# Seven products in the first up-projection pair of MLP groups 2 to 6, with low parts taken from a copy in PSUM

## The chip, the cores and the metric

The kernel runs on one core of one Trainium2 chip. The metric is the time of one execution on the device in microseconds; before the change three runs gave 1218.8, 1220.0 and 1220.02, with a median of 1220.0. The engines of the core are named as the profile names them: PE (TensorE: matmuls), PEld (its weight loads), DVE (VectorE), ACT (ScalarE), POOL (GpSimd) and SP (SyncE, which issues the loads).

## The reference

The program computes two layers of a decoder trunk on 512 tokens of width 1024, in float32. Layer 0 mixes tokens by attention with a forget gate, layer 1 by a gated short convolution. Each mixer is followed by a squared-ReLU MLP of inner width 4096 and by a gated embedding; RMSNorm stands around every part.

```python
D_MODEL = 1024; SEQ = 512; DEPTH = 2; D_FF = 4 * D_MODEL

def sq_relu_mlp(h, w_up, w_down):
    return jnp.square(jax.nn.relu(h @ w_up)) @ w_down

# in each layer i
x = x + rmsnorm(m, g[1])                                  # m: the mixer
f = sq_relu_mlp(rmsnorm(x, g[2]), w_mlp_up[i], w_mlp_down[i])
x = x + rmsnorm(f, g[3])
```

## The kernel before

**Split operands.** Each float32 operand is held as two tiles of a rounded type: `hi`, the value rounded by a cast on ScalarE (line 276), and `lo`, the rest, a subtraction on VectorE or GpSimd (line 277). One product is three matmuls into the same PSUM bank (`mm3`, lines 268 to 270): hi by hi, lo by hi, hi by lo. A weight tile of 128 x 512 thus costs a load, a cast and a subtraction before TensorE can use it.

**Groups.** The 4096 inner columns of an MLP are eight groups of 512. A group has four blocks f = 0 to 3 of 128 inner columns. Up: block f is 8 k steps of `mm3` with 512 moving columns (the tokens), 24 matmuls; ScalarE takes Relu and Square of the bank (lines 975 and 961). Group 0 does this in two halves of 256 tokens, since the tokens of its second half come out of the norm later. Down, in groups 0 to 6: seven products in place of eight, after Strassen and Winograd. `PRODUCTS` names the operand pairs, and `STEPS = (1, 2, 4, 5, 6, 7, 3)` their order. A operands (A11, A12, A22, S1 to S4) come from the squared blocks: blocks 0 and 1 give the parts p = 0, blocks 2 and 3 the parts p = 1. S1 and S2 share a tile, S3 and S4 another; their sums are GpSimd's (line 989), their casts ScalarE's, their low parts VectorE's. B operands are raw `w_down` tiles and the sums T1 to T4 of them; the sums are GpSimd's (line 168), and so are the low parts of T tiles from group 1 on. Each product has two banks, added to SBUF accumulators by VectorE (line 1021). Group 7 is plain.

**Weights.** All weight tiles stand in one list in the order of use. `prepare(upto)` issues the work for the list up to a place; a use of a tile calls it for `SOON` = 8 places ahead. Raw tiles arrive through a ring of 14 by DMAs on SP's queue; SBUF tiles of one size come from a ring of 70 pages, and PSUM is eight banks of 128 x 512.

**Order.** The program text is input to a scheduler that sets the order on each engine from its own estimates; only stretches under `manual_schedule` stand as written. On each engine the instructions run strictly in that order.

**Norm and convolution.** `pre_norm` computes statistics, scales the tokens, and puts off their transposition; then TensorE transposes into banks (`n_p`, line 337), ScalarE casts them into `hTh` and VectorE makes `hTl`. Between layer 0 and the convolution a function `quarters` copies each bank once more into float32 pages `B11`, `B21`, `B12`, `B22` (line 1242), from which the convolution makes token sums T1 to T4: its own projections c and b already run as seven products, with 256 moving columns (`sevens`).

## Time and profile before

| | |
|---|---|
| median of three runs | 1220.0 us (1218.8 to 1220.02) |
| span of the profiled execution, first to last instruction | 1216.5 us |
| around the span, to the median | 3.5 us |
| granted TensorE clock, mean | 0.999 |
| busy: PE, PEld | 1205.5, 1027.5 us |
| busy: DVE, ACT, POOL | 931.4, 691.4, 655.4 us |
| read from HBM | 139.03 MB |

The profile is of one execution, and its span is the profiled execution's own time as far as it is recorded; the runs' median is the time from outside. Busy time is the union of an engine's instructions. A matmul's end is modelled, and matmuls overlap: their cost is the distance between the starts of neighbours. In a group line the name left of the arrow is the tile that is written, right of it those that are read, without buffer numbers; then come count, total, mean in ns, and idle time before with what ended it. A timeline line gives start, length, engine, line, operation, tiles, count and, in brackets, the idle time before it and its releaser; a line with a count over 1 is a run of equal instructions.

### The profile page before, as it was taken

The numbers are of one execution on the slowest core, as the hardware profiler recorded it, in microseconds if no ns is written. First come the engines' busy times: TensorE is split into PE (matmuls) and PEld (weight loads), VectorE is DVE, ScalarE is ACT, GpSimd is POOL, SyncE is SP. The second block draws the span as 40 slices with busy tenths as digits, with TensorE's granted clock in tenths as the row PEclk, the third lists the DMA queues.
The fourth block names the chain that finished last, engine by engine and source line by source line (L and its number), as shares of the span: only waits on it lengthen the run. The fifth ranks groups of instructions, "written<-read, shape, count | busy, mean of one in ns | idle before, by whom it ended". The sixth has DMA issues, their size and how long they took to land.

```text
span 1216.5 us, 18743 instructions
## 1 busy us (share of the span) xinstructions
PE 1205.5 (99%) x6175; PEld 1027.5 (84%) x6175; DVE 931.4 (77%) x1474; ACT 691.4 (57%) x1465; POOL 655.4 (54%) x616
## 2 busy tenths in 40 slices
PE   9999999999999999999999999999999999999997
PEld 8888887898888888888889999989888888888886
DVE  7888889586669766879877888866876787669873
ACT  7687778458644564455665534545746445645551
POOL 2035666155787877774213455126676878678210
PEclk9999999999999999999999999999999999999999
DMA  9376544623234323438223123542422443135401
GB/s 333 122 210 172 167 152 125 222 93 94 77 113 138 102 66 110 139 97 276 83 88 108 35 80 103 176 154 71 139 87 65 127 138 106 61 112 185 162 13 58
DMA packets 87314, 150.84 MB, mean 124 GB/s; under 512 B 10352, under 2 KB 18080, under 8 KB 87216
## 3 DMA queue, kind: packets, MB, share of 16 engines
q1 hardware_dynamic: 86640, 149.11, 39.3%
q8 instruction: 49, 0.80, 0.3%
q10 hardware_dynamic: 576, 0.53, 0.1%
q14 instruction: 49, 0.40, 0.1%
HBM read 139.03 MB, written 6.37 MB: 120 GB/s over the span
## 4 chain that ended last, share of the span: by engine, by line
PE 91%; ACT 3%; issue 2%; DVE 2%; POOL 1%; DMA 0%; SPq 0%; POOLq 0%; DVEq 0%; ACTq 0%
PE up L269 9%; PE up L270 9%; PE up L268 9%; PE dn L268 8%; PE dn L270 8%; PE dn L269 8%; PE v L476 3%; PE pg L269 2%; PE pg L268 2%; PE pg L270 2%; PE qk L270 2%; PE qk L269 2%; PE qk L268 2%; PE pT L590 1%; PE co L269 1%
## 5 line engine op out<-in xcount | busy, mean ns | idle before, releaser
L277 DVE TENSOR_TENSOR wl<-raw,wh 128x512 fp32r<-128x512 f32 x346 | 344.7, 1041 | 14.1 <-ACT wh L276 13.4
L269 PE MATMUL up<-hTh,wl 128*128 128x512 f32 (+1 forms) x576 | 210.2, 365 | 0.0
L270 PE MATMUL up<-hTl,wh 128*128 128x512 f32 (+1 forms) x576 | 209.6, 365 | 0.0
L268 PE MATMUL up<-hTh,wh 128*128 128x512 f32 (+1 forms) x576 | 208.7, 366 | 0.0
L276 ACT CAST wh<-raw 128x512 fp32r<-128x512 f32 x346 | 189.4, 625 | 4.5 <-DVE xd L373 4.4
L975 ACT ACTIVATE r<-up 128x512 f32<-128x512 f32 (+1 forms) x72 | 39.5, 548 | 201.8 <-PE up L270 190.1
L277 POOL TENSOR_TENSOR wl<-dn_T,wh 128x512 fp32r<-128x512 f32 x96 | 132.7, 1416 | 30.0 <-ACT wh L276 30.0
L168 POOL TENSOR_TENSOR dn_T<-raw,raw 128x512 f32<-128x512 f32 x56 | 87.0, 1564 | 69.1 <-DMA raw<-in_wdn 50.5
L269 PEld LDWEIGHTS up<-hTh,wl 128*128 128x128 f32 x576 | 108.6, 189 | 17.5
L268 PEld LDWEIGHTS up<-hTh,wh 128*128 128x128 f32 x576 | 108.6, 189 | 17.5
L270 PEld LDWEIGHTS up<-hTl,wh 128*128 128x128 f32 x576 | 108.2, 189 | 17.4
L1021 DVE TENSOR_TENSOR acc<-dn,acc 128x512 f32<-128x512 f32 x168 | 107.4, 680 | 13.9 <-PE dn L270 13.9
L168 POOL TENSOR_TENSOR dn_T<-raw,dn_T 128x512 f32<-128x512 f32 x56 | 92.5, 1651 | 2.2
L276 ACT CAST wh<-dn_T 128x512 fp32r<-128x512 f32 x112 | 61.4, 616 | 10.9 <-POOL dn_T L168 10.9
L277 DVE TENSOR_TENSOR A12l<-q,A12h 128x512 fp32r<-128x512 f32 x28 | 23.2, 829 | 53.8 <-ACT A12h L276 53.8
L1035 POOL TENSOR_TENSOR acc<-acc,acc 128x512 f32<-128x512 f32 x28 | 46.9, 1707 | 9.9 <-DVE acc L1021 9.9
L277 DVE TENSOR_TENSOR A11l<-q,A11h 128x256 fp32r<-128x256 f32 x28 | 23.2, 828 | 36.5 <-ACT A11h L276 36.5
L270 PE MATMUL qk<-hTl,wh 128*128 128x512 f32 x128 | 50.7, 396 | 0.0
L269 PE MATMUL pg<-wh,hTl 128*128 128x512 f32 x128 | 50.5, 394 | 0.0
L268 PE MATMUL pg<-wh,hTh 128*128 128x512 f32 x128 | 50.4, 394 | 0.0
L268 PE MATMUL qk<-hTh,wh 128*128 128x512 f32 x128 | 50.3, 393 | 0.0
L269 PE MATMUL qk<-hTh,wl 128*128 128x512 f32 x128 | 50.2, 392 | 0.0
(404 smaller groups left out, 3304.5 us busy)
## 6 DMA issues: line engine op xcount, KB each, us to landing
raw<-in_wup SPq DMA_DIRECT2D x128, 256.0 KB, 2.9
raw<-in_wdn SPq DMA_DIRECT2D x128, 256.0 KB, 2.8
raw<-in_wcq SPq DMA_DIRECT2D x36, 256.0 KB, 2.8
raw<-in_wqk SPq DMA_DIRECT2D x32, 256.0 KB, 5.3
raw<-in_wpg SPq DMA_DIRECT2D x32, 256.0 KB, 4.1
g<-in_g SPq DMA_DIRECT2D x22, 256.0 KB, 5.9
prl<-neg_c SPq DMA_DIRECT2D x16, 256.0 KB, 6.3
raw<-in_wo SPq DMA_DIRECT2D x16, 256.0 KB, 4.7
```

The source lines that it names most:

```text
L168: ins = nc.gpsimd.tensor_tensor(out=B[name], in0=B[a], in1=B[b], op=op)
L268: nc.tensor.matmul(ps, a.hi, b.hi, start=start, stop=False)
L269: nc.tensor.matmul(ps, a.lo, b.hi, start=False, stop=False)
L270: nc.tensor.matmul(ps, a.hi, b.lo, start=False, stop=stop)
L276: nc.scalar.copy(hi, src)
L277: return eng.tensor_tensor(out=lo, in0=src, in1=hi.bitcast(F32), op=ALU.subtract)
L476: nc.tensor.matmul(ps[:, : V_CHUNKS[c][1]], getattr(of_x(k, t), p), getattr(ready["v", c, k], of), start=k == 0 and p == of, stop=k == KT ...
L590: nc.tensor.transpose(ps[:, b * P : (b + 1) * P], probs[h][b][:, j * P : (j + 1) * P], ident)
L975: nc.scalar.activation(r[:, :n], ps[:, :n], AF.Relu)
L1021: ins = nc.vector.tensor_tensor(out=a, in0=banks[s], in1=a, op=ALU.add)
L1035: nc.gpsimd.tensor_tensor(out=a, in0=a, in1=acc[i, s][:, :S], op=ALU.add)
```

## The change

In groups 2 to 6 of both layers blocks 0 and 1 of the up-projection are one product of a 1024 x 256 weight and the 1024 x 512 tokens, done as seven products of halves: seven times 4 k steps of `mm3` with 256 moving columns. The weight's forms are A11, A12, A22 raw and S1 to S4, summed by GpSimd with low parts on VectorE; the tokens' forms are quarters of hT and T1 to T4. The T tiles are made once per layer: `quarters` now also runs with the norm ahead of each MLP, and GpSimd subtracts, ScalarE casts and VectorE splits in groups 0 and 1, a step at a time between products. Two of the three banks are put together by four additions on VectorE, the third by ScalarE's half copy and one of them; `crossed` makes the A operands of the pair in its new layout.

In the same groups a weight's low part on VectorE is taken from a second rounded copy, which ScalarE writes to one of two PSUM banks (`beside`), kept for the rest of the layer's groups; S forms are left plain. T4 and T1 of `w_down` change from GpSimd to VectorE. The order of the T sums changes in all groups. Within groups 2 to 6 TensorE's order is as written, and the distance of preparation is set by hand. Pages are 77 in place of 70. The layout of the up weights of these pairs is permuted on the host.

```diff
-PAGES = 70
+PAGES = 77
+BESIDE = range(2, 7)
+ON_VECTOR = ("T4", "T1")
+PLAINLY = {("up", "S1"), ("up", "S2"), ("up", "S3"), ("up", "S4")}
+FIXED = range(2, 7)
+BACK = 6
+UP_SEVENS = range(2, 7)
+MORE = 0
+UP_FORMS = ("A11", "S2", "S1", "S3", "A12", "S4", "A22")
...
                 ((name, p), (a, p), (b, p), ALU.subtract)
+                for these in (
+                    (("T1", "B12", "B11"), ("T2", "B22", "T1"), ("T4", "B21", "T2")),
+                    (("T3", "B22", "B12"),),
+                )
                 for p in range(2)
-                for name, a, b in (("T1", "B12", "B11"), ("T3", "B22", "B12"),
-                                   ("T2", "B22", "T1"), ("T4", "B21", "T2"))
+                for name, a, b in these
...
                 eng = nc.gpsimd if (key[0] == "dn" and key[2] > 0) or key[-1] in ON_POOL else nc.vector
+                if key[0] == "up" or near(key) and key[3] in ON_VECTOR:
+                    eng = nc.vector
...
+            elif near(key) and eng is nc.vector and (key[0], key[-1]) not in PLAINLY:
+                split_beside(hi[:, :w], lo[:, :w], raw[:, :w], key[1])
             else:
                 split(hi[:, :w], lo[:, :w], raw[:, :w], eng)
...
+    def split_beside(hi, lo, src, l):
+
+        n = besides[l, "n"] = 1 - besides.get((l, "n"), 1)
+        if (l, n) not in besides:
+            besides[l, n] = bank(f"beside{l}_{n}")
+        copy = besides[l, n][:, : src.shape[-1]]
+        nc.scalar.copy(copy.bitcast(F32R), src)
+        nc.scalar.copy(hi, src)
+        nc.vector.tensor_tensor(out=lo, in0=src, in1=copy, op=ALU.subtract)
...
+                    if f < 2 and gr in UP_SEVENS:
+                        if f == 0:
+                            done(f, 0, S, *up_sevens(gr))
+                        continue
...
+                    if gr == 1:
+                        next(aside, None)
+                    if gr in FIXED:
+                        prepare(where["up", l, 2 * gr + 1, 3] + 1 + (SOON if f == 3 else SOON - BACK + 2))
...
+        def token_sums():
+            for name, a, b in (("T1", "B12", "B11"), ("T2", "B22", "T1"),
+                               ("T3", "B22", "B12"), ("T4", "B21", "T2")):
+                for q in range(2):
+                    full[name, q] = page(f"{name}f{l}_{q}")
+                    t = full[name, q][:, :S]
+                    nc.gpsimd.tensor_tensor(
+                        out=t, in0=full[a, q][:, :S], in1=full[b, q][:, :S], op=ALU.subtract
+                    )
+                    T[name, q] = Pair(*(page(f"{name}{s}{l}_{q}", F32R) for s in "hl"))
+                    split(T[name, q].hi[:, :S], T[name, q].lo[:, :S], t)
+                    yield
...
+        def up_sevens(gr):
+            L, R = slice(0, S // 2), slice(S // 2, S)
+            a, b, c = (bank(f"up{l}_{gr}_{s}") for s in "abc")
+            u, v, d, m = (page(f"u{s}{l}_{gr}") for s in "uvdm")
...
+            product(c[:, L], "A11", "B11")
+            nc.scalar.copy(u[:, L], c[:, L])
+            product(a[:, R], "S2", "T2")
+            product(b[:, L], "S1", "T1")
+            product(b[:, R], "S3", "T3")
+            product(a[:, L], "A12", "B21")
...
+            add(two(d[:, :S]), two(a), both(u[:, L]))
+            add(two(v[:, :S]), two(b), both(d[:, R]))
+            add(d[:, R], b[:, L], v[:, R])
+            product(c[:, L], "S4", "B22")
+            product(c[:, R], "A22", "T4")
+            add(m[:, :S], c, v[:, :S])
...
             for i in STEPS:
+                next(aside, None)
...
-            up(gr, done)
-            down(gr, A)
+            with ExitStack() as order:
+                if gr in FIXED:
+                    order.enter_context(tc.manual_schedule(engines={mybir.EngineType.PE}))
+                up(gr, done)
+                down(gr, A)
...
-            kind, lhs, xs, g1, lambda t: pre_norm(t, xs[t], g2, hT, f"n2{l}"), opened
+            kind, lhs, xs, g1, lambda t: pre_norm(t, xs[t], g2, hT, f"n2{l}", quarters), opened
```

**ScalarE at the end of the up-projection of group 5, layer 0.** `r`, `q` are Relu and Square of a block (the third number is f), `A11h` to `S3h` the casts of A operands, `wh` the casts of weights with the number of the place in the list; `dn_0_5_T4_1` is T4, p = 1. Before:

```order
L276 CAST wh190_6073<-dn_0_5_T4_0_5969 128x512
L276 CAST wh191_6083<-dn_0_5_T4_1_5977 128x512
L276 CAST wh192_6093<-dn_0_5_T1_0_5963 128x512
L276 CAST wh193_6103<-dn_0_5_T1_1_5971 128x512
L975 ACTIVATE r0_5_2_0_6113<-up0_5_2_0_6072 128x512
L961 ACTIVATE q0_5_2_5944<-r0_5_2_0_6113 128x512
L276 CAST A11h0_5_2_6116<-q0_5_2_5944 128x256
L975 ACTIVATE r0_5_3_0_6147<-up0_5_3_0_6122 128x512
L961 ACTIVATE q0_5_3_5945<-r0_5_3_0_6147 128x512
L276 CAST A12h0_5_3_6150<-q0_5_3_5945 128x512
L276 CAST S1h0_5_3_6158<-s120_5_3_6154 128x512
L276 CAST S3h0_5_3_6162<-s340_5_2_6120 128x512
```

Now:

```order
L1016 ACTIVATE r0_5_2_0_6508<-up0_5_2_0_6483 128x512
L996 ACTIVATE q0_5_2_6282<-r0_5_2_0_6508 128x512
L295 CAST A11h0_5_2_6511<-q0_5_2_6282 128x256
L1016 ACTIVATE r0_5_3_0_6542<-up0_5_3_0_6517 128x512
L996 ACTIVATE q0_5_3_6283<-r0_5_3_0_6542 128x512
L295 CAST A12h0_5_3_6545<-q0_5_3_6283 128x512
L295 CAST S1h0_5_3_6553<-s120_5_3_6549 128x512
L295 CAST S3h0_5_3_6557<-s340_5_2_6515 128x512
L311 CAST wh202_6561<-dn_0_5_T4_0_6371 128x512
L311 CAST wh203_6566<-dn_0_5_T4_1_6377 128x512
```

The casts of T4 and T1 stood ahead of block 2's Relu; now they stand behind block 3's last cast. Their copies to PSUM (not shown) stand ahead of the pair's Relus.

**VectorE at the same place, now.** `wl202` is the low part of T4, p = 0.

```order
L296 TENSOR_TENSOR A12l0_5_3_6546<-q0_5_3_6283,A12h0_5_3_6545 128x512
L1138 TENSOR_TENSOR acc0_1_1_4166<-dn0_5_11_6582,acc0_1_1_4166 128x512
L296 TENSOR_TENSOR S1l0_5_3_6554<-s120_5_3_6549,S1h0_5_3_6553 128x512
L296 TENSOR_TENSOR S3l0_5_3_6558<-s340_5_2_6515,S3h0_5_3_6557 128x512
L312 TENSOR_TENSOR wl202_6562<-dn_0_5_T4_0_6371,beside0_0_4698 128x512
```

These low parts of T4 were GpSimd's before; now they follow the last low part of the A operands on VectorE.

**ScalarE at the entry of the convolution.** `n0b_p` are the banks of the transposed tokens, `wh268` to `wh271` (`wh283` to `wh286` now) the weights of the second c and u, `cs` the first copy behind. Before:

```order
L276 CAST wh268_7869<-raw226_7871 128x512
L276 CAST wh269_7881<-raw227_7883 128x512
L276 CAST wh270_7893<-raw228_7895 128x512
L276 CAST hTh_84<-n0b_p2_0_7994 128x4x128
L276 CAST hTh_84<-n0b_p2_1_8005 128x4x128
L276 CAST wh271_7905<-raw229_7907 128x512
L276 CAST hTh_84<-n0b_p3_0_8016 128x4x128
L276 CAST hTh_84<-n0b_p3_1_8025 128x4x128
L927 COPY cs0_0_7942<-c0_0_7868 128x256
```

Now:

```order
L295 CAST hTh_84<-n0b_p2_0_8498 128x4x128
L295 CAST wh283_8373<-raw226_8375 128x512
L295 CAST hTh_84<-n0b_p2_1_8509 128x4x128
L295 CAST wh284_8385<-raw227_8387 128x512
L295 CAST hTh_84<-n0b_p3_0_8520 128x4x128
L295 CAST wh285_8397<-raw228_8399 128x512
L295 CAST hTh_84<-n0b_p3_1_8529 128x4x128
L295 CAST wh286_8409<-raw229_8411 128x512
L962 COPY cs0_0_8446<-c0_0_8372 128x256
```

Three of the four weight casts stood ahead of all the token casts; now one stands behind each token cast.

87 lines of the change are left out of this document (67 added, 20 removed).

## Prediction

> **What bounds the kernel now.** First I read the page: busy time by engine, and the chain that ended last.
>
> ```profile
> PE 1205.5 (99%) x6175; PEld 1027.5 (84%) x6175; DVE 931.4 (77%) x1474; ACT 691.4 (57%) x1465; POOL 655.4 (54%) x616
> PE 91%; ACT 3%; issue 2%; DVE 2%; POOL 1%; DMA 0%; SPq 0%; POOLq 0%; DVEq 0%; ACTq 0%
> ```
>
> Matmul spans overlap, so 99% alone proves little; the chain with 91% TensorE says more. Then I read the stages: two stretches of one steady group each in layer 0. The columns are length, then busy time (count) of PE, PEld, DVE, ACT and POOL, then clock, DMA share and GB/s.
>
> ```profile
> 399.00:440.00 41.00, 41.00 (x183) 33.96 (x182) 29.55 (x36) 21.03 (x39) 32.76 (x26) 1.00 0.33 104
> 440.00:481.00 41.00, 41.00 (x183) 33.96 (x182) 28.94 (x36) 21.03 (x39) 31.07 (x25) 1.00 0.34 103
> ```
>
> TensorE has no idle time here and its full clock, DMA is at a third, ScalarE at half and VectorE and GpSimd near three quarters. In groups 2 to 6, then, only fewer or cheaper matmuls shorten the kernel, as long as no other engine becomes late. What a matmul really costs is the distance between starts, read from the timeline: two starts 24 matmuls apart for 512 columns, and two starts 36 apart for 256.
>
> ```profile
> 433.84 0.39 PE L270 MATMUL up<-hTl,wh 128*128 128x512 f32 x1
> ...
> 439.28 0.39 PE L270 MATMUL up<-hTl,wh 128*128 128x512 f32 x1
> 439.51 0.39 PE L268 MATMUL dn<-wh,A11h 128*128 128x512 f32 x1
> ...
> 700.03 0.28 PE L268 MATMUL c_A<-T4h,wh 128*128 128x256 f32 x1
> ...
> 704.35 0.28 PE L268 MATMUL b_S<-T2h,wh 128*128 128x256 f32 x1
> ```
>
> 5.44 / 24 = 0.2267 us for 512 columns; 4.32 / 36 = 0.120 us for 256. A group has 96 matmuls up and 84 down: 180 x 0.2267 = 40.8 us.
>
> **The columns.** In ten groups (2 to 6, two layers) the first pair drops 48 matmuls of 512 columns and gains 84 of 256: 48 x 0.2267 - 84 x 0.120 = 10.88 - 10.08 = 0.80 us less. Seven eighths of the products would be 1.36 us; 256 columns cost more than half of 512, and that takes 0.56 back. Ten groups: **-8.0 us**. The 256-column rows are from the convolution's seven products, the same shape, with T tiles and with hT, and across a change of bank.
>
> **The work on the other engines.** The costliest groups of instructions give their prices, and three timeline rows the prices back to back.
>
> ```profile
> L277 DVE TENSOR_TENSOR wl<-raw,wh 128x512 fp32r<-128x512 f32 x346 | 344.7, 1041 | 14.1 <-ACT wh L276 13.4
> L276 ACT CAST wh<-raw 128x512 fp32r<-128x512 f32 x346 | 189.4, 625 | 4.5 <-DVE xd L373 4.4
> L1021 DVE TENSOR_TENSOR acc<-dn,acc 128x512 f32<-128x512 f32 x168 | 107.4, 680 | 13.9 <-PE dn L270 13.9
> L277 POOL TENSOR_TENSOR wl<-dn_T,wh 128x512 fp32r<-128x512 f32 x96 | 132.7, 1416 | 30.0 <-ACT wh L276 30.0
> L168 POOL TENSOR_TENSOR dn_T<-raw,dn_T 128x512 f32<-128x512 f32 x56 | 92.5, 1651 | 2.2
> ...
> 446.41 7.39 ACT L276 CAST wh<-raw 128x512 fp32r<-128x512 f32 x14
> 460.93 3.00 POOL L168 TENSOR_TENSOR dn_T<-raw,raw 128x512 f32<-128x512 f32 x2
> 463.83 5.21 DVE L277 TENSOR_TENSOR wl<-raw,wh 128x512 fp32r<-128x512 f32 x4
> ```
>
> Back to back a cast is 7.39 / 14 = 0.53 us, and a low part with both inputs in SBUF, beside GpSimd, 5.21 / 4 = 1.30. Each group's changes:
> - VectorE: three more low parts and four more from GpSimd (T4 and T1). Seventeen now read PSUM, 0.68 each by the accumulations' row, where ten cost 1.04: 17 x 0.68 - 10 x 1.04 = +1.2. The four S parts stay in SBUF: 4 x 1.04 = +4.2, less the four plain parts they replace, -4.2. Four additions from PSUM, +2.5. About 33 us of 40.
> - ScalarE: 17 copies and three casts, 20 x 0.53 = +10.6, and one half copy; 32 of 40.
> - GpSimd: four S sums, 4 x 1.65 = +6.6, less four low parts, 4 x 1.42 = -5.7; 33 of 40.
>
> All three fit below 40.0, so throughput costs nothing; the matmuls cover it, and without that cover VectorE's or GpSimd's 33 would be the bound. Two PSUM banks are held from group 2 on. Six remain; the seven products use three, a down product two, drained in 2 x 0.68 while the next takes 12 x 0.2267 = 2.7: free. DMA bytes are the same; SP's loads, at a third of the DMA time, cover a reordering. What remains is lateness in the queues.
>
> **T4's wait, each group.** T4's and T1's casts, ahead of block 2's Relu before, now stand behind S3h of block 3, and T4's low parts behind S3l on VectorE. The timeline of ScalarE and VectorE after the last up matmul (issue ends at 439.51):
>
> ```profile
> 439.71 0.60 ACT L975 ACTIVATE r<-up 128x512 f32<-128x512 f32 x1 [2.48 <-PE up L270]
> 441.00 0.62 ACT L276 CAST A12h<-q 128x512 fp32r<-128x512 f32 x1
> 442.98 0.62 ACT L276 CAST S1h<-s 128x512 fp32r<-128x512 f32 x1 [1.35 <-POOL s L989]
> 443.80 0.62 ACT L276 CAST S3h<-s 128x512 fp32r<-128x512 f32 x1 [0.20 <-POOL s L989]
> 444.33 2.18 ACT L276 CAST wh<-dn_T 128x512 fp32r<-128x512 f32 x4
> ...
> 445.45 1.42 DVE L277 TENSOR_TENSOR S3l<-s,S3h 128x512 fp32r<-128x512 f32 x1
> ```
>
> Product 4 starts 24 matmuls later, at 439.51 + 5.44 = 444.95. Its high part, cast at 444.33 in 0.62, lands at 444.95: just in time. The low part is used two matmuls later, at 445.40. S3h is there at 444.42; S3l takes 0.68 and blocks VectorE for 0.60 if GpSimd is quiet; T4's low part then runs from 445.05 to 445.73. TensorE waits 0.33 us, and everything down the group is queued behind. The ends: 0 if ScalarE runs earlier, and 1.0 if S3l takes 1.42 as in its row. I take 0.33, since GpSimd then waits for T2's cast, which stands still further back: 10 x 0.33 = **+3.3**. A12, wanted at 439.51 + 18 x 0.2267 = 443.59, is cast by 441.62 and its low part follows: covered.
>
> **Group 0, each layer.** The token sums need sixteen more ScalarE copies out of the transposes' banks. The first eight fall into ScalarE's wait for the norm (3.80 in the first row). The last eight stand behind block 2, and four banks stay taken.
>
> ```profile
> 255.91 0.64 ACT L312 ACTIVATE junk<-xb 128x512 f32<-128x512 f32 x1 [3.80 <-DVE xb L373]
> ...
> 268.89 3.18 POOL L168 TENSOR_TENSOR dn_T<-raw,dn_T 128x512 f32<-128x512 f32 x2
> 272.10 1.66 ACT L276 CAST wh<-dn_T 128x512 fp32r<-128x512 f32 x3 [5.71 <-POOL dn_T L168]
> 273.66 0.37 ACT L975 ACTIVATE r<-up 128x256 f32<-128x256 f32 x1
> ...
> 269.59 0.28 PE L268 MATMUL up<-hTh,wh 128*128 128x256 f32 x1
> ```
>
> ScalarE waits for T4's second half, GpSimd's eighth sum. The new order of the sums makes it the sixth, so block 2's Relu moves with it by 3.18, from 273.66 to 270.5. The block of matmuls that starts at 269.59 (48 x 0.120 before down) now needs that Relu's bank, free at 270.9, since the transposes' banks come later still, behind eight copies: **+1.3**, twice 2.6. Ends: 0 and 1.3 + 2.1, all eight copies (8 x 0.265: in the rows below two copies start 0.53 before the next two) on the path. The sixteen splits of the T tiles on ScalarE and VectorE and GpSimd's eight subtractions have groups 0 and 1 to hide in, product by product.
>
> **The convolution's entry.** Its source is the same, but ScalarE's order moved: three of the four weight casts that ran before the last transposes now stand between the hT casts.
>
> ```profile
> 649.41 1.65 ACT L276 CAST wh<-raw 128x512 fp32r<-128x512 f32 x3
> 652.94 1.08 ACT L276 CAST hTh<-n0b_p 128x512 fp32r<-128x512 f32 x2 [1.89 <-PE n0b_p L337]
> ...
> 657.73 0.68 ACT L1242 COPY B12f<-n0b_p 128x256 f32<-128x256 f32 x2
> 658.26 0.70 ACT L1242 COPY B22f<-n0b_p 128x256 f32<-128x256 f32 x2
> ```
>
> 1.65 us of filler leaves idle time and enters the path: **+1.6** (0 if TensorE has other work, 2.1 if all four casts count).
>
> **The sum.** -8.0 + 3.3 + 2.6 + 1.6 = -0.5 on a span of 1216.5. The runs' median, 1220.0, lies 3.5 above the span, so **1219.5 us**. This kernel's measurement tells nothing within about 0.2% (2.4 us) from no change.
>
> **The rivals.**
> *Relief, faster.* VectorE's low parts take one input from PSUM; if that frees GpSimd, whose sums take 1.65 us in the mean but 1.50 each in the row at 460.93, beside accumulations, ScalarE waits less for S1 and T4, and T4's and group 0's waits vanish: -8.0 + 1.6 = -6.4, **1213.6**. For it: the accumulations stay at 0.68 beside the same GpSimd. Against it: half of T4's wait is ScalarE's own chain, which GpSimd enters only once.
> The Trainium skill's page "ScalarE: Activation LUTs", section "Step-by-step: what each stage is for", holds that ScalarE writes faster to PSUM than to SBUF, with the caveat that TensorE should not need most of PSUM. No run here shows such a write; by that rule this rival gains, by the caveat the next one.
> *ScalarE late, slower.* The place is its queue from the first of the seven products to block 3's Relu. In 10.08 + 48 x 0.2267 = 20.96 us it does twenty copies and casts (10.6), a half copy and two Relus and Squares for the pair (2.7), the stretch from A12h to behind S3h (441.00 to 444.33 in the rows above, GpSimd's sums included: 3.3), and block 2's Relu, Square and A11 cast (1.7): 18.3, slack 2.7. Each copy into the two banks also waits until VectorE has read the one before. If the four S parts take 1.30 in place of 0.60 (+2.8) and 13 PSUM copies 0.625 in place of 0.53 (+1.2), the slack is overdrawn by 1.3 us, and from there each microsecond goes straight into T4's wait: 1219.5 + 13 = **1232.5**. For it: the 1.30 row. Against it: each of the rest reads PSUM.
> *The products don't shrink.* If weight loads set the pace at 1027.5 / 6175 = 0.166 us, the pair would cost 84 x 0.166 = 13.9, 3.1 more than now: **1258**. The 0.120 rows speak against it.
>
> **How the numbers follow.** Forecast 0.41, relief 0.30, ScalarE late 0.27, no shrinking 0.02. Each has its spread: relief in part ends inside the 0.2%, the forecast's own ends reach outside. Faster 0.31, same 0.40, slower 0.29. The forecast's own range is 1216 to 1223; the range for 8 in 10 reaches to relief and to most of late ScalarE: 1213 to 1231.
>
> **What would show it.** Groups 2 to 6 should take 40.3 us each, with a hole of some 0.3 us on TensorE two matmuls into product 4, released by VectorE's low part. No hole at all, and GpSimd's sums near 1.3, would be relief. Holes at the first product's second half, or at S4's product (which waits until ScalarE has copied the bank's left half), and Relu of block 3 starting late, would be late ScalarE. Group 0 should show a wait of PE for a Relu near its third late block, and the convolution's entry an idle stretch of 1 to 2 us before the second c and u. A pitch over 0.120 in the products would refute the first term; TensorE idle for raw tiles from DMA would refute what I hid.

## The result, and the profile after

The changed kernel takes **1255.4 us** (median of four runs, 1253.8 to 1256.5) against 1220.0: a ratio of **1.0296**, 95% interval 1.0281 to 1.031. It is 35 us slower; the forecast was 1219.5, with a range of 1213 to 1231. The profiled execution has a span of 1254.8, 38.3 more than before.

The page of the changed kernel, busy time by engine and the chain that ended last:

```profile
PE 1219.3 (97%) x6535; PEld 1039.1 (83%) x6535; DVE 959.6 (76%) x1600; ACT 814.9 (65%) x1723; POOL 669.6 (53%) x632
PE 51%; DVE 14%; ACT 12%; POOL 11%; issue 8%; DMA 3%; POOLq 0%; SPq 0%; DVEq 0%; ACTq 0%
```

No engine became the bound: the fullest after TensorE (PE and its weight loads) is VectorE at 76%. But PE's share of the chain fell from 91% to 51%: it now waits in turn for three engines that are each idle for about a quarter of the time or more. To find where, I read the start of each group's first up matmul from the timelines of both kernels and took the lengths between them:

| stretch (us) | before | after | difference | forecast |
|---|---|---|---|---|
| start to group 0, layer 0 | 250.6 | 252.2 | +1.6 | 0 |
| groups 0 to 3, layer 0 | 167.2 | 181.2 | +14.0 | +0.4 |
| groups 4 to 6, layer 0 | 122.4 | 124.5 | +2.1 | -1.4 |
| group 7 to layer 1's group 0 | 278.9 | 283.2 | +4.3 | +1.6 |
| groups 0 to 3, layer 1 | 166.7 | 179.6 | +12.9 | +0.4 |
| groups 4 to 6, layer 1 | 122.4 | 125.6 | +3.2 | -1.4 |
| group 7, layer 1, to the end | 108.4 | 108.5 | +0.1 | 0 |

(The forecast column is the prediction's terms put into these stretches: per layer 1.3 for group 0, and per group of 2 to 6 0.33 less 0.80.) So 27 of the 38 us are lost in groups 0 to 3, 22 of them in groups 0 and 1, before the first seven products are reached. The windows view, first of before for groups 0 and 1, then of after for groups 0, 1 and 4, with the columns as in the prediction:

```profile
250.60:295.30 44.70, 44.57 (x293) 40.20 (x292) 30.57 (x38) 29.16 (x65) 23.17 (x23) 1.00 0.22 73
295.30:333.90 38.60, 38.60 (x172) 31.95 (x172) 29.38 (x32) 27.15 (x51) 30.24 (x24) 1.00 0.35 107
```

```profile
252.20:303.30 51.10, 45.74 (x293) 40.28 (x292) 40.02 (x44) 39.07 (x93) 34.86 (x30) 1.00 0.18 57
303.30:349.10 45.80, 42.57 (x182) 33.36 (x181) 23.59 (x37) 23.25 (x44) 40.69 (x29) 1.00 0.30 93
...
433.40:475.00 41.60, 41.16 (x218) 34.69 (x217) 32.39 (x48) 31.28 (x59) 28.93 (x25) 1.00 0.32 100
```

Group 0 does the same 293 matmuls in 51.1 us instead of 44.7, and VectorE, ScalarE and GpSimd each have some ten us more there. In group 1 PE idles 3.2 us while VectorE and ScalarE are idle for half of it; GpSimd is shown busy for 40.7 of 45.8 us, which the experiments take apart. (Before, two us of group 2 are drawn forward into group 1, so its 38.6 compare with about 40.8.) What PE waited for in the changed kernel, in total, times, and longest:

```profile
PE dn L289 <- DVE wl L296: 7.1, 8, 1.1
PE dn L287 <- ACT wh L311: 3.0, 10, 0.6
...
PE dn L287 <- ACT A11h L295: 2.5, 2, 1.4
PE up L287 <- ACT r L1016: 2.5, 4, 1.5
```

The first row, eight waits for plain low parts, is group 0's products with S1 and S3; the second, ten waits, one in each group with seven products; the last is the wait forecast for group 0. Behind some of these waits TensorE's granted clock falls as well (last section).

### The profile page after: what moved, and what is told of

It is laid out like the page before. It is cut to its first block, busy times and chain, and to the rows that moved or that the text cites. A ratio compares the mean times of both kernels' runs of the same rounds, so it can differ in the third digit from the quotient of the medians.

```text
span 1254.8 us, 19832 instructions
## 1 busy us (share of the span) xinstructions
PE 1219.3 (97%) x6535; PEld 1039.1 (83%) x6535; DVE 959.6 (76%) x1600; ACT 814.9 (65%) x1723; POOL 669.6 (53%) x632
## 4 chain that ended last, share of the span: by engine, by line
PE 51%; DVE 14%; ACT 12%; POOL 11%; issue 8%; DMA 3%; POOLq 0%; SPq 0%; DVEq 0%; ACTq 0%
PE dn L289 4%; PE dn L288 4%; PE dn L287 4%; DVE wl L312 4%; POOL s L1091 3%; DVE wl L296 3%; POOL dn_T L179 3%; POOL s L1108 3%; DVE acc L1138 3%; PE v L511 2%; PE qk L289 2%; PE qk L288 2%; PE qk L287 2%; ACT q L996 2%; DMA raw<-in_wup 2%
## 5 line engine op out<-in xcount | busy, mean ns | idle before, releaser
L296 DVE TENSOR_TENSOR wl<-raw,wh 128x512 fp32r<-128x512 f32 x206 | 173.7, 884 | 10.7 <-ACT wh L295 10.4
L287 PE MATMUL up<-hTh,wh 128*128 128x512 f32 (+1 forms) x416 | 148.1, 358 | 2.5 <-ACT r L1016 2.5
L288 PE MATMUL up<-hTh,wl 128*128 128x512 f32 (+1 forms) x416 | 147.8, 357 | 0.0
L289 PE MATMUL up<-hTl,wh 128*128 128x512 f32 (+1 forms) x416 | 147.3, 356 | 0.0
L310 ACT CAST beside<-raw 128x512 fp32r<-128x512 f32 x130 | 74.9, 587 | 40.5 <-DVE wl L312 38.5
L312 DVE TENSOR_TENSOR wl<-raw,beside 128x512 fp32r<-128x512 f32 x130 | 84.3, 679 | 12.6 <-ACT beside L310 11.4
L296 POOL TENSOR_TENSOR wl<-dn_T,wh 128x512 fp32r<-128x512 f32 x56 | 71.7, 1314 | 40.0 <-ACT wh L295 40.0
L287 PEld LDWEIGHTS up<-hTh,wh 128*128 128x128 f32 x416 | 78.6, 189 | 14.4 <-ACT r L1016 3.3
L288 PEld LDWEIGHTS up<-hTh,wl 128*128 128x128 f32 x416 | 78.6, 189 | 10.9
L296 DVE TENSOR_TENSOR A11l<-q,A11h 128x256 fp32r<-128x256 f32 (+1 forms) x28 | 21.2, 759 | 51.7 <-ACT A11h L295 51.7
L296 DVE TENSOR_TENSOR wl<-up_S,wh 128x512 fp32r<-128x512 f32 x40 | 51.2, 1293 | 0.0
```

The lines of the kernel that those rows point to most:

```text
L287: nc.tensor.matmul(ps, a.hi, b.hi, start=start, stop=False)
L288: nc.tensor.matmul(ps, a.lo, b.hi, start=False, stop=False)
L289: nc.tensor.matmul(ps, a.hi, b.lo, start=False, stop=stop)
L296: return eng.tensor_tensor(out=lo, in0=src, in1=hi.bitcast(F32), op=ALU.subtract)
L310: nc.scalar.copy(copy.bitcast(F32R), src)
L312: nc.vector.tensor_tensor(out=lo, in0=src, in1=copy, op=ALU.subtract)
```

## The experiments

The theory at the start (A): the token sums, which I had priced at nothing, cost most of it, in groups 0 and 1. The rival (B): the steady groups, with ScalarE late. All times below are medians against 1219.3 to 1219.7 for the kernel before on the same chip (1220.0 for the changed kernel); the last three columns are read as in the table above, the groups as the sum of both layers, in the kernel's profiled execution.

| kernel | us | ratio, 95% interval | groups 0-3 | groups 4-6 | between layers |
|---|---|---|---|---|---|
| before | 1219.3 to 1219.7 | 1 | 333.9 | 244.8 | 278.9 |
| changed | 1255.4 | 1.0281 to 1.031 | 360.8 | 250.1 | 283.2 |
| order_only | 1221.1 | 1.0005 to 1.0023 | 332.5 | 244.8 | 281.8 |
| beside_only | 1222.3 | 1.0014 to 1.0033 | 332.6 | 242.6 | 283.6 |
| sevens_free | 1230.2 | 1.0071 to 1.0102 | 335.6 | 250.0 | 283.3 |
| sums_only | 1248.0 | 1.022 to 1.025 | 358.0 | 244.8 | 283.6 |
| sevens_only | 1331.1 | 1.0901 to 1.0934 | 387.3 | 299.5 | 282.5 |
| copies_only | 1234.4 | 1.011 to 1.014 | 342.5 | 244.8 | 282.1 |
| copies_own | 1222.2 | 1.0011 to 1.0031 | 335.8 | 244.8 | 280.1 |
| sums_nosplit | 1234.8 | 1.011 to 1.0144 | 346.2 | 244.8 | 283.3 |
| casts_only | 1235.7 | 1.0108 to 1.0145 | 346.6 | 244.8 | 283.3 |
| lows_pool | 1256.8 | 1.0293 to 1.0324 | 367.5 | 244.8 | 282.1 |
| sums_vector | 1251.4 | 1.0252 to 1.0291 | 359.1 | 248.7 | 281.9 |
| splits_later | 1253.0 | 1.0251 to 1.0286 | 358.4 | 250.9 | 282.7 |
| vector_later | 1247.0 | 1.0203 to 1.0235 | 351.3 | 249.9 | 281.8 |
| all_group1 | 1260.5 | 1.0318 to 1.0349 | 367.2 | 251.1 | 282.7 |
| from3 | 1261.2 | 1.0326 to 1.0357 | 367.7 | 248.6 | 281.8 |
| beside_all | 1262.6 | 1.034 to 1.0375 | 372.2 | 248.1 | 283.3 |
| after_own | 1247.1 | 1.0209 to 1.0241 | 357.7 | 249.0 | 280.4 |
| own_vector_later | 1241.2 | 1.0165 to 1.0199 | 350.0 | 249.2 | 279.8 |

### Which part of the change costs

**The token sums alone.**

```diff
-UP_SEVENS = range(2, 7)
+UP_SEVENS = range(0)
-BESIDE = range(2, 7)
+BESIDE = range(0)
-FIXED = range(2, 7)
+FIXED = range(0)
```

with the old order of GpSimd's weight sums.

> The kernel before, with the sixteen copies of the turned tokens and the eight token sums per layer with their splits made and thrown away: plain products and plain splits everywhere, and the old order of GpSimd's weight sums. Theory A (the token sums, made in groups 0 and 1, cost most of the 35 us, because GpSimd's sums there hold up VectorE's low parts and VectorE's stream then holds up GpSimd): the changed kernel's own marks moved by 13.0 and 12.2 us over groups 0 and 1 of the two layers, so this one loses some 20 to 27 us, 1240 to 1247 us, and a GpSimd sum of over 5 us stands in group 1. Rival B (the steady groups with the seven products and the second copy lose it, ScalarE being late): nothing of theirs is in it, so it loses no more than the 2.6 us forecast for group 0 and some 3 us at the convolution's entry, 1220 to 1226 us.

Measured 1248.0, just above theory A's range. Copies, sums and splits that nothing uses cost 28 us in a kernel that is otherwise the one before but for its ring of 77 pages, and all of it lies in groups 0 to 3 and around them; groups 4 to 6 are to the tenth as before. A GpSimd sum of over 8 us is there too.

**Seven products and token sums without the second copy.**

```diff
-BESIDE = range(2, 7)
+BESIDE = range(0)
```

> The changed kernel without the second rounded copy in PSUM: all low parts are made from the two SBUF inputs as before, and the T4 and T1 weight sums and the seven products' sums keep their engines of before where the new branch does not ask for VectorE. Theory A: the token sums' 25 us stay, the steady groups come within 2 us of the changed kernel's either way, 1240 to 1265 us. Rival B: ScalarE loses 130 copies of 0.59 us, which is 76 us of its work, and the steady groups fall from 41.5 to 40.3 us, so about 12 us come back, 1238 to 1245 us, with groups 0 and 1 unchanged at 12 us lost.

Both were wrong: 1331.1. The second copy does not slow the sevens down, it carries them; without it groups 2 to 5 take 48 to 50 us each and group 6 takes 52.7, and PE waits in each for ScalarE's cast of A11. ScalarE is late there because it waits for VectorE's additions (the second row, from group 4 of layer 0, where ScalarE is busy for 23.2 of 49.2 us):

```profile
PE dn L287 <- ACT A11h L295: 30.9, 10, 3.1
...
464.87 0.63 ACT L1077 ACTIVATE rd<-ud 128x512 f32<-128x512 f32 x1 [12.04 <-DVE ud L1053]
```

The edit also gives the low parts of T4 and T1 back to GpSimd, so the run does not test the second copy alone.

**The second copy alone.**

```diff
-UP_SEVENS = range(2, 7)
+UP_SEVENS = range(0)
-FIXED = range(2, 7)
+FIXED = range(0)
-        aside = token_sums()
+        aside = iter(())
```

and no copies of tokens.

> The kernel before with the second rounded copy alone: VectorE's low parts of groups 2 to 6 read PSUM, no seven products in the up-projection, no copies of tokens and no token sums. Theory A: 0 to 4 us faster or the same, 1214 to 1222 us, since PE was 97 per cent busy and sets the steady groups' 40.8 us. Rival B: ScalarE's added copies make high parts late in each group, 0.5 to 1.2 us in each of ten groups, 1225 to 1232 us.

1222.3, between the two. The groups are no longer than in order_only; what it lost lies between the layers and goes with the next run, not with ScalarE. (Of its 283.6 there 1.8 are group 7's, whose first matmuls are drawn forward into group 6.)

**What is left of the edit.** As the last one, with BESIDE empty as well.

> The changed kernel's file with no seven products, no second copy, no copies of tokens and no token sums: what is left are the new order of GpSimd's four weight sums for the down-projection, 77 pages instead of 70 and the smaller scratch for transfers. It prices the rest of the edit. Both theories hold it to be nothing: within 2 us of before, 1218 to 1222 us. If it were the cause of the 3 to 5 us lost between the layers, 1223 to 1226 us.

1221.1, as expected, though not quite nothing. Groups 0 to 3 even gain 1.4 us over both layers, and 2.9 are lost between them, at the convolution's entry, where ScalarE's order is that of the changed kernel (more on it below). All kernels with a ring of 77 pages have 281.8 to 283.6 there, those with 69 pages (below) 279.8 to 280.4, the one before, with 70, 278.9. That the ring brings the order is suggested by this list, and no run has isolated it. Beside_only aside, every kernel above 282.1 has a stretch at half the granted clock in this part, and no other has one.

**Sevens and second copy without the token sums.**

```diff
-                return T[name, k // 2].at(lambda u: u[:, k % 2 * 256 : k % 2 * 256 + 256])
+                return hT.at(lambda u: u[:, k, : S // 2])
-        aside = token_sums()
+        aside = iter(())
```

and no copies of tokens. The sums are left out, so the result of the up-projection is another.

> The changed kernel without the copies and the token sums: the products with T1 to T4 read the first half of the first four chunks of the turned tokens in their place (left out: the sums, so the up-projection's result is another). Everything of groups 2 to 6 stays. If groups 0 and 1 alone lose what the ladder says, groups 0 and 1 come back to the 82 us of the run with the new order alone, the steady groups keep 41.4 to 41.6 us against 40.8, and it takes 1225 to 1233 us. If the steady groups themselves are held up by what groups 0 and 1 leave late, they fall to 40.3 us as forecast, 1214 to 1219 us.

1230.2. Taken as steps from the kernel before to the changed one, the 35 us are 1.4 for the order, 1.2 more for the second copy (the two intervals overlap), 7.9 more for the seven products, and 25.1 more for the token sums with their copies. What speaks for the last step is that it comes out alike in two kernels: in groups 0 to 3 the token sums cost 360.8 - 335.6 = 25.2 us in the changed kernel, and 358.0 - 333.9 = 24.1 without any seven products, with the old order of the weight sums. Two questions remain: what in the token sums costs 25 us, and why a steady group takes 41.5 and not 40.3.

### The token sums, step by step

**The copies.** From sums_only, with the sums left undone:

```diff
-        aside = token_sums()
+        aside = iter(())
```

> The first step of a ladder up to the run with the token sums alone (1247.95 us): the kernel before with the sixteen copies of the turned tokens on ScalarE per layer, nothing made of them. Both theories: the changed kernel entered group 0 1.6 us later and its group 0 waited 1.65 us for a bank behind the copies, so 2 to 4 us per layer, 1222 to 1227 us.

1234.4: sixteen copies per layer of some 0.3 us each cost 15 us, where both theories gave 2.5 to 7.5. The timeline of this kernel, PE first, then ScalarE:

```profile
272.53 0.28 PE L286 MATMUL up<-hTl,wh 128*128 128x256 f32 x1
276.52 0.39 PE L284 MATMUL up<-hTh,wh 128*128 128x256 f32 x1 [3.71 <-ACT r L1013]
...
262.33 2.05 ACT L292 CAST hTh<-n_p 128x512 fp32r<-128x512 f32 x4 [2.45 <-PE n_p L369]
...
274.53 1.66 ACT L292 CAST wh<-dn_T 128x512 fp32r<-128x512 f32 x3 [5.60 <-POOL dn_T L176]
276.10 0.38 ACT L1013 ACTIVATE r<-up 128x256 f32<-128x256 f32 x1
...
277.26 0.64 ACT L1331 COPY B12f<-n_p 128x256 f32<-128x256 f32 x2
```

The four banks of the transposes are read by the casts at 262.33, and ScalarE could be done with them at 264.4. The copies read them as well, and stand in ScalarE's queue at 277.26, behind casts that wait 5.60 us for GpSimd. So four of eight banks stay taken for some 13 us more, PE runs out of banks at 272.6, and what it then waits for is a Relu in that same queue. ScalarE waited for GpSimd before too (5.71 us in the prediction's row); with eight banks PE did not feel it. Behind this hole the granted clock is at half from 277.9 to 281.3, so group 0 loses more than the hole: it takes 49.9 us in place of 44.7.

**The same copies, early.**

```diff
-                full[at] = page(f"{at[0]}f{q}")
+                full[at] = normed.tile([P, S], F32, tag=f"{at[0]}f{q}", name=f"{at[0]}f{q}_{l}")
-PAGES = 77
+PAGES = 69
```

> The run with the copies alone, but the copies go to eight pages of their own instead of pages of the ring (which has 69 then instead of 77). In ScalarE's queue the second half's eight copies then stand right behind the casts that read the same four PSUM banks, and no longer behind four weight casts that wait 5.6 us for GpSimd. Theory of the banks (the copies, late in the queue, hold four of eight banks from 262 to 278 us, so PE has to wait 3.9 us for a Relu that stands in that queue too): the hole of 3.9 us goes, group 0 comes from 49.9 back to 44 to 46 us, 1222 to 1228 us. Rival (ScalarE's time for sixteen copies, wherever they stand, or the ring of pages): 1231 us or more.

1222.2: 12 of the 15 us are back. ScalarE's timeline of this kernel:

```profile
262.66 0.66 ACT L1331 COPY B12f<-n_p 128x256 f32<-128x256 f32 x2
...
274.44 1.66 ACT L292 CAST wh<-dn_T 128x512 fp32r<-128x512 f32 x3 [4.50 <-POOL dn_T L176]
276.00 0.38 ACT L1013 ACTIVATE r<-up 128x256 f32<-128x256 f32 x1
```

The same Relu is as late as in the last run (276.00 against 276.10), and PE waits for no Relu any more: with the copies right behind the casts the banks are free. It is the banks, and not ScalarE's time, that cost. (Order and ring change together in this run; the rows speak for the order.)

**The sums, without their splits.** From sums_only:

```diff
-                    T[name, q] = Pair(*(page(f"{name}{s}{l}_{q}", F32R) for s in "hl"))
-                    split(T[name, q].hi[:, :S], T[name, q].lo[:, :S], t)
                     yield
```

> The second step of the ladder: copies and GpSimd's eight token sums per layer, no casts and no low parts of them. Theory of the shared memory port (a GpSimd sum and VectorE's low parts take turns, 1.73 us for the pair instead of 0.60 and 1.29): eight sums cost VectorE about 9 us per layer where it has none to spare, so half or more of the ladder's 28 us is here, 1234 to 1243 us. Theory of ScalarE's order (a cast that waits for its sum holds the casts and copies behind it): no cast waits for a sum here, so at most 2 us above the copies alone, 1224 to 1229 us, and the third step, the splits, costs the rest.

1234.8: GpSimd's eight sums add 0.4 us to the copies by the medians (2.5 by the spans of the two profiled executions). The theory of the shared memory, in this form, falls: half of the 28 us was to be here. That 1234.8 lies in its range is luck, since the copies alone cost more than both theories gave.

**The casts, without the low parts.** From sums_only:

```diff
-                    split(T[name, q].hi[:, :S], T[name, q].lo[:, :S], t)
+                    nc.scalar.copy(T[name, q].hi[:, :S], t)
```

> Between the ladder's second step (copies and sums, 1234.8 us) and its third (with casts and low parts, 1248.0 us): the eight casts per layer on ScalarE, without VectorE's eight low parts. If ScalarE's order is the price (each cast waits for its sum and holds two weight casts and two accumulator copies behind it): 1244 to 1248 us. If it is VectorE (eight more operations with two SBUF inputs where GpSimd's sums and weight low parts take turns already): 1235 to 1239 us.

1235.7: 0.9 more. So the last step of the ladder, eight low parts of 0.6 us per layer on VectorE, costs the other 12 us.

**The low parts on GpSimd.** From sums_only:

```diff
-                    split(T[name, q].hi[:, :S], T[name, q].lo[:, :S], t)
+                    split(T[name, q].hi[:, :S], T[name, q].lo[:, :S], t, nc.gpsimd)
```

> The run with the token sums alone (copies, sums, casts and low parts, unused: 1248.0 us), the eight low parts per layer by GpSimd instead of VectorE. If VectorE's own queue is the price (three low parts per product there at up to 1.73 us each, 5.2 us against 2.72 us of PE), VectorE is back to two per product, the holes of 3.0 us at S1 and S3 in group 0 shrink below 1.2 us and the time falls to 1236 to 1241 us. If it is the shared memory, whoever makes them, or GpSimd's queue, in which the weight sums of group 1 now stand behind eight more operations, nothing or less than 3 us is gained: 1245 to 1255 us.

1256.8, the rival, and above its range. VectorE had its two low parts per product again, and group 0 fell from 53.6 to 51.7 us; but group 1 rose from 41.9 to 48.5. The timelines of the three say why. Casts only, VectorE, GpSimd and ScalarE:

```profile
297.92 19.52 DVE L293 TENSOR_TENSOR wl<-raw,wh 128x512 fp32r<-128x512 f32 x14
...
302.34 1.42 POOL L176 TENSOR_TENSOR dn_T<-raw,raw 128x512 f32<-128x512 f32 x1 [1.49 <-PE dn L286]
...
317.99 1.47 POOL L1029 TENSOR_TENSOR T4f<-B21f,T2f 128x512 f32<-128x512 f32 x1
...
319.49 0.62 ACT L1033 CAST T4h<-T4f 128x512 fp32r<-128x512 f32 x1 [5.46 <-POOL T4f L1029]
```

All token sums, low parts on VectorE:

```profile
297.90 3.46 DVE L293 TENSOR_TENSOR wl<-dn_T,wh 128x512 fp32r<-128x512 f32 x2
...
309.11 3.70 DVE L293 TENSOR_TENSOR wl<-raw,wh 128x512 fp32r<-128x512 f32 x6
...
305.76 9.43 POOL L176 TENSOR_TENSOR dn_T<-raw,raw 128x512 f32<-128x512 f32 x2 [4.95 <-DVE T3l L293]
...
323.76 1.29 POOL L1029 TENSOR_TENSOR T4f<-B21f,T2f 128x512 f32<-128x512 f32 x1
...
325.08 0.62 ACT L292 CAST T4h<-T4f 128x512 fp32r<-128x512 f32 x1 [8.46 <-POOL T4f L1029]
325.60 0.59 ACT L1013 ACTIVATE r<-up 128x512 f32<-128x512 f32 x1
```

Low parts on GpSimd:

```profile
313.79 3.44 POOL L176 TENSOR_TENSOR dn_T<-raw,raw 128x512 f32<-128x512 f32 x2
...
327.45 1.26 POOL L1029 TENSOR_TENSOR T4f<-B21f,T2f 128x512 f32<-128x512 f32 x1
...
328.75 0.62 ACT L292 CAST T4h<-T4f 128x512 fp32r<-128x512 f32 x1 [10.60 <-POOL T4f L1029]
```

The last of the eight token sums stands on GpSimd behind the eight weight sums of group 1, and its cast on ScalarE in front of the second Relu of group 1. The cast starts 16.2, 19.2 and 25.8 us after group 1's first matmul (303.29, 305.87 and 302.98), and group 1 takes 38.9, 41.9 and 48.5 us: us for us. The low parts put GpSimd's weight sums back: on GpSimd they stand ahead of them (the sums begin at 313.8 in place of 302.3), and beside them on VectorE the first of the sums takes 8.2 us (last section). The token sum moves with the weight sums, then its cast, the Relu, and what stands behind that: A12's cast, the casts of group 1's weight sums and GpSimd's low parts of these. PE feels it in the down part of group 1, by 4.44 us at A12's cast in lows_pool, and by 1.1 at GpSimd's low parts in both kernels that are late. The rest, in group 0, is VectorE: with three low parts per product at up to 1.73 us each (the 3.46 for two above) against 2.72 us of PE, PE waits there for plain low parts, 5.1 us in sums_only over both layers.

The changed kernel has the same rows, GpSimd and ScalarE:

```profile
302.76 8.65 POOL L179 TENSOR_TENSOR dn_T<-raw,raw 128x512 f32<-128x512 f32 x1 [4.49 <-PE dn L288]
...
322.86 0.62 ACT L295 CAST T4h<-T4f 128x512 fp32r<-128x512 f32 x1 [8.82 <-POOL T4f L1032]
323.39 0.59 ACT L1016 ACTIVATE r<-up 128x512 f32<-128x512 f32 x1
```

The Relu at 323.39 stands behind a cast that waits 8.82 us and whose result nobody needs before group 2.

### Other places for the same steps

**The sums on VectorE.** From the changed kernel:

```diff
-                    nc.gpsimd.tensor_tensor(
+                    nc.vector.tensor_tensor(
                         out=t, in0=full[a, q][:, :S], in1=full[b, q][:, :S], op=ALU.subtract
```

> The changed kernel with the eight token sums per layer computed by VectorE instead of GpSimd, all else as it is. Theory A in its narrow form (the two engines hold each other up at the memory they share, two-input sums on GpSimd against two-input low parts on VectorE): the four holes of 4.2 us in all at group 0's products with S1 and S3 shrink below 1.5 us, the GpSimd sum of 8.65 us falls below 3 us, and 10 to 22 us come back, 1233 to 1245 us. The rival (it is the amount of work in groups 0 and 1, above all ScalarE's casts in their place in its queue): under 5 us come back, 1250 us or more.

1251.4: of the narrow theory's two signs both came (PE waits for no low part at S1 and S3, and the sum of 8.65 us is gone), and of its 10 to 22 us only 4, which is the rival's figure. Now ScalarE waits for VectorE's sum in each step:

```profile
290.27 0.62 ACT L295 CAST T1h<-T1f 128x512 fp32r<-128x512 f32 x1 [0.55 <-DVE T1f L1032]
...
293.46 0.62 ACT L295 CAST T2h<-T2f 128x512 fp32r<-128x512 f32 x1 [0.56 <-DVE T2f L1032]
```

3.19 us from step to step, where PE needs 2.72 for a product. Group 0 falls to 47.3, group 1 rises to 49.0.

**The splits in group 1.** Eight sums in group 0, then two splits after each block of group 1:

```diff
                 next(aside, None)
+                if i == STEPS[0]:
+                    next(aside, None)
...
                     if gr == 1:
                         next(aside, None)
+                        next(aside, None)
```

with `token_sums` giving first all sums, then all splits.

> The changed kernel with GpSimd's eight token sums still stepped through group 0's products (all eight there now), but their casts and low parts only in group 1, two after each of its four up-projection blocks. Two mechanisms for the four holes of 4.2 us at group 0's products with S1 and S3 are told apart. If it is ScalarE's order (a cast that waits for its sum stands ahead of the product's two weight casts and two copies; with the sums on VectorE such a step took 3.19 us against 2.72 us of a product), the holes go and group 0 comes down from 51 to about 47 us. If it is the memory that VectorE and GpSimd share (weight low parts at 1.73 us instead of 0.60 while a token sum runs, two of them per product), the holes stay at 3 to 4 us. Either way the T4 cast no longer stands ahead of group 1's Relus, which is worth up to 7 us per layer: 1236 to 1248 us.

1253.0, above the range. Group 0 falls to 48.6 and keeps 1.8 us of holes at S1 and S3, half of what it had: both mechanisms are in them. Group 2 then waits for what group 1 has not done, 46.6 instead of 42.8 us.

**The same, sums on VectorE.** From the last run:

```diff
-                    nc.gpsimd.tensor_tensor(
+                    nc.vector.tensor_tensor(
```

> As the run with the later splits, but the eight sums by VectorE in group 0. Neither of the two mechanisms has a place in group 0 here: no cast waits for a sum there and GpSimd is still, so both theories want group 0 within 1.5 us of the 44 us of before plus the 2 us of its copies, with no hole over 0.4 us at S1 and S3. What is left of the loss in group 1 tells what the splits cost there: 1228 to 1240 us. If more than 15 us per layer pair stay lost in groups 0 and 1, both mechanisms are too small and the casts' and low parts' sheer amount is the cause.

1247.0, above the range. Group 0 is as forecast by both, 45.6 us with no hole at S1 or S3. But groups 1 and 2 take 43.3 and 45.6, and 8.4 us are won where 15 or more were to be.

**Everything in group 1.**

```diff
-                next(aside, None)
                 a_name, b_name = PRODUCTS[i]
...
                         next(aside, None)
+                        next(aside, None)
```

> The changed kernel with all of the token sums, casts and low parts in group 1, two whole steps after each up-projection block, none in group 0. Theory of ScalarE's order: group 0 comes back to about 46 us (the copies alone), and group 1 becomes the slow one, since its Relus now stand behind casts that wait for GpSimd's sums, which stand behind eight weight sums: group 1 at 50 us or more, 1248 to 1262 us. Rival (the amount of work decides, and group 1 has room, as ScalarE has no accumulator copies there): both groups together lose under 4 us per layer, 1230 to 1240 us.

1260.5, as the theory of ScalarE's order had it: 51.0 us in group 1, and 46.6 in group 0.

**Sevens from group 3, steps in groups 1 and 2.**

```diff
-UP_SEVENS = range(2, 7)
+UP_SEVENS = range(3, 7)
...
-                    if gr == 1:
+                    if gr in (1, 2):
                         next(aside, None)
...
-                next(aside, None)
                 a_name, b_name = PRODUCTS[i]
```

> The changed kernel with seven products from group 3 instead of 2, and the token sums stepped one after each up-projection block of groups 1 and 2, none in group 0: half of them now run where VectorE's low parts read PSUM. If room is what counts (groups 0 and 1 have none on VectorE and ScalarE, the steady groups have 9 us on each), groups 0 to 3 fall from 181 to 171 to 174 us per layer: 1234 to 1243 us. If the order of the steps counts (each a round trip of sum, cast and low part in front of a Relu), each of the eight steps costs 1.5 us wherever it stands: 1248 us or more.

1261.2, the rival. Room does not help: half of the steps now stand in group 2, of a kind in which VectorE and ScalarE are idle for a quarter of the time or more (26.0 and 30.6 of 40.8 us busy in beside_only), and group 2 takes 50.0 us.

**The second copy in groups 0 and 1 too.**

```diff
-BESIDE = range(2, 7)
+BESIDE = range(0, 7)
```

> The changed kernel with the second rounded copy in PSUM in groups 0 and 1 too, so that VectorE's low parts of weights there no longer read two SBUF operands. Theory of the port: VectorE's low parts stay at 0.6 to 0.7 us beside GpSimd's sums, the stretch of 8.65 us is gone, and groups 0 to 3 fall from 181 to about 172 us per layer, 1235 to 1246 us. Theory of ScalarE: it gets some 30 more copies of 0.59 us in groups 0 and 1 of each layer, 18 us, in the order that already held them up: groups 0 to 3 rise to 185 us or more, 1260 to 1290 us.

1262.6, as the theory of ScalarE had it. PE's longest waits are for banks again, two of which are now the copies':

```profile
PE n_p L372 <- ACT r L1016: 8.7, 2, 4.4
PE up L287 <- ACT r L1016: 6.5, 2, 4.2
```

### The two findings put to use

**Copies in pages of their own, in the changed kernel.** The edit of copies_own:

```diff
-                full[at] = page(f"{at[0]}f{q}")
+                full[at] = normed.tile([P, S], F32, tag=f"{at[0]}f{q}", name=f"{at[0]}f{q}_{l}")
```

> The changed kernel with the copies in eight pages of their own, the ring having 69 pages. Theory of the banks: the hole of 1.65 us in group 0 goes and the loss before it shrinks, 3 to 8 us back in both layers together, 1247 to 1252 us, since here the hole was already smaller than in the run with the copies alone. Rival (the ring of pages is what is short, since sixteen pages of split token sums live through five groups): eight pages fewer in it cost more than that gains, 1256 us or more.

1247.1, 8.3 us back, at the edge of what was expected: 3.1 in groups 0 to 3, 2.8 between the layers, 1.4 ahead of group 0, 1.1 in groups 4 to 6.

**With later splits and the sums on VectorE as well**, the edits of vector_later on top:

```diff
-                    nc.gpsimd.tensor_tensor(
+                    nc.vector.tensor_tensor(
...
                     if gr == 1:
                         next(aside, None)
+                        next(aside, None)
```

> The changed kernel with what the runs found put right as far as possible: copies in pages of their own (8.3 us in the changed kernel), the eight sums by VectorE in group 0 and the splits after group 1's blocks (8.4 us). If the two are separate causes they add up: 1255.4 - 8.3 - 8.4 = 1238.7, so 1236 to 1242 us. If they were the same loss counted twice (PE waiting in groups 0 and 1 for whatever comes last), no more than 2 us is gained over the better one: 1244 to 1248 us. Not below 1230 us in either case, which is what the steady groups cost without any token sums.

1241.2 for the 1238.7 of the sum: 14.2 of the 25 us that the token sums cost are back, and the two causes are mostly separate. It is the best form of the change that was run, and still 1.8% slower than the kernel before. With 1230 for the sevens without any token sums, I do not expect any placing of these alone to win.

## Why the prediction was wrong

**The step that failed** is the price of the token sums: 2.6 us for their copies, and nothing for the rest, because the sixteen splits of the T tiles and GpSimd's eight subtractions "have groups 0 and 1 to hide in, product by product". Together they cost 25 of the 35 us. Alone in the kernel before, the copies cost 15, and the sums, casts and low parts that were priced at nothing 13.5 more. How the 25 us of the changed kernel divide between the two is not isolated; 8.3 come back when only the copies move, 8.4 when only the sums and splits do, 14.2 with both. I looked at room, in the steady groups (33, 32 and 33 us of 40), and for these steps neither at the room in groups 0 and 1 nor at order. The steps are round trips of GpSimd, ScalarE and VectorE, spliced into queues that run strictly in order, with Relus and weight casts behind them; the ladder shows that sums and casts by themselves cost 1 us, and the low parts 12 or 21, by the queue in which they make others late. The part of my own working that asks what is queued behind a wait was done for T4's weights and for the copies, and not for the sums and splits.

**Group 0's copies.** Place and mechanism were right: PE waits for a Relu behind block 2, with four banks still taken. Forecast 1.3, measured 1.65 in layer 0 of the changed kernel (the earlier GpSimd sum does help: 3.9 without it); in layer 1 PE waits there twice, 0.33 each. But the banks had a second price that I did not look for; after_own gave 8.3 us in all where the term had 2.6, though the 2.8 of them between the layers may be the ring's, and some 1.3 of these the clock's, since after_own has no stretch at half clock there.

**The columns.** Right: 84 matmuls of 256 columns took 10.1 us, 132 of 512 columns 29.9, so 40.0 for a group without holes. The 0.80 us a group were there to be had.

**T4's wait** is the second term that was mis-sized. The place was right. PE in the last but one steady group of layer 0, then ScalarE:

```profile
497.33 0.40 PE L287 MATMUL dn<-wh,A11h 128*128 128x512 f32 x1
497.83 0.50 PE L288 MATMUL dn<-wh,A11l 128*128 128x512 f32 x1
...
501.63 0.40 PE L289 MATMUL dn<-wl,A12h 128*128 128x512 f32 x1
502.30 0.51 PE L287 MATMUL dn<-wh,A11h 128*128 128x512 f32 x1 [0.27 <-ACT wh L311]
502.64 0.39 PE L288 MATMUL dn<-wh,A11l 128*128 128x512 f32 x1
503.10 0.50 PE L289 MATMUL dn<-wl,A11h 128*128 128x512 f32 x1
...
494.08 0.62 ACT L295 CAST S1h<-s 128x512 fp32r<-128x512 f32 x1 [2.06 <-POOL s L1108]
...
495.43 0.59 ACT L1016 ACTIVATE r<-up 128x512 f32<-128x512 f32 x1
...
501.11 0.62 ACT L295 CAST S3h<-s 128x512 fp32r<-128x512 f32 x1 [0.53 <-POOL s L1091]
501.63 1.65 ACT L311 CAST wh<-dn_T 128x512 fp32r<-128x512 f32 x3
```

Beyond the 0.23 of a matmul PE is late by 0.27 at product 1's second half, by 0.44 at T4's high part and by 0.23 at its low part, and each hole makes the matmul after it 0.11 longer: 1.3 us a group, where I had 0.33. Block 2's matmuls end at 490.5 (24 of 0.2267 before the start of down at 495.97), and its Relu starts at 495.43, behind S1h, which waited 2.06 us for GpSimd; so A11's second half is late, and S3h comes 5.1 us after the up matmuls instead of 4.3. This is the **rival of late ScalarE**, with the hole at the first product's second half that it named. Its first condition came too: the low parts of the S forms, which it put at 1.30 us in place of 0.60, take 1.32 in the mean of groups 4 to 6 of layer 0. With the forecast's 0.33 it priced 1.63 us a group; the ten groups of sevens_free take 41.6 us in the mean, 1.6 over the 40.0. The rival without the copies' 2.6 gives 1229.9, and the changed kernel without the token sums took 1230.2; that the totals meet so closely is in part luck, since 4.4 us were lost between the layers where 1.6 were forecast. The row that spoke for this rival was in the prediction.

**Throughput** was right: 33, 32 and 33 us a group were forecast for VectorE, ScalarE and GpSimd; the window at 433.40 has 32.4, 31.3 and 28.9. **Relief** came in its premise and not in its effect: in groups 4 to 6 of layer 0 GpSimd's weight sums take 1.30 us in beside_only and 1.56 to 1.63 in order_only, and the kernel is no faster, as PE had no idle time in these groups to give back. With the seven products they take 1.41 to 1.53, and the holes are there.

**The convolution's entry**: 1.6 forecast, 4.3 measured between the layers. Order_only has 2.9 of these, with no copy or sum moved but with the order of ScalarE's casts that the forecast named. The wait comes through VectorE, though, which makes the low parts of these weights behind the late casts and between those of the tokens. PE in order_only:

```profile
656.77 0.39 PE L288 MATMUL c<-hTh,wl 128*128 128x256 f32 x1 [1.12 <-DVE wl L296]
...
658.47 0.38 PE L288 MATMUL c<-hTh,wl 128*128 128x256 f32 x1 [0.72 <-DVE wl L296]
```

The kernel before has one such wait, of 0.28. So the place was right, the path was another, and no run has changed this order alone. The other 1.4 us are about what the granted clock takes behind the same two waits in the changed kernel (last section).

## What to carry to other kernels

Work that is to hide in idle time has to be priced by what stands behind it in each in-order queue that it passes: find the consumer that is due first, and put a round trip (sum, cast, low part) behind that, not in front. A second reader of a PSUM bank lengthens its life to that reader's place in the queue; with eight banks, a wait that was harmless on ScalarE comes through to TensorE. Before costing a part at nothing, build the kernel with that part alone and its result unused: one run would have shown the 28 us.
